# Moving blocks of conditioning work between the stages of a two-layer backbone kernel, with the conv's end started two jobs later, the gate row in another memory bank, and the output written in half as many stores

## The chip, the cores and the metric

The kernel runs on one core of a Trainium2 chip. The time is the device time of one execution in microseconds (us); lower is better. A core has five engines with a queue each: PE (TensorE, matrix products), DVE (VectorE), ACT (ScalarE), POOL (GpSimd) and SP (SyncE, which here only issues DMA transfers). An instruction waits at the head of its engine's queue until what it needs is there, and all behind it wait too.

## The reference

Two layers work on 256 latent tokens of width 2048, one sample. A conditioning vector c gives shift, scale and gate of each layer:

```
mod = silu(c) @ ada_w[layer] + ada_b[layer]          # 2048 -> 3 * 2048
shift, scale, gate = split(mod, 3)
h = rmsnorm(x, norm_g[layer]) * (1 + scale) + shift
# layer 0
k, v, q, za, glu, zb = split(h @ w_in)               # q, k: RMS norm and rotary
attn = attention of 8 query heads over latent and context keys
conv = silu(layernorm(depthwise_conv_31(a * sigmoid(b))))   # glu = a, b
x = x + gate * (concat(attn * silu(za), conv * silu(zb)) @ w_out0)
# layer 1
u, v, z = split(h @ w_in1);  x = x + gate * ((u * mix(layernorm(v)) * silu(z)) @ w_out1)
return rmsnorm(x, final_g)
```

All is fp32. The weights are far larger than the data of 256 tokens: 241 MB are read in one run.

## The kernel before, in words

**Jobs.** The work is a list of jobs (`plan`). A W job takes one piece of a weight matrix: 512 KB are loaded by SP into a buffer `raw`, ACT rounds it to `whi` (L389), DVE or, for the W jobs 30 to 133, POOL takes the rest `wlo = raw - whi` (L392), and PE multiplies both parts with both parts of the data, three products for each tile (`w_rows`, `w_cols`). In `w_cols` a job is twelve matmuls of 128x512. An adaLN vector of layer 0's shift and scale comes from PE (`araw`, L345).

**Conditioning blocks.** Gate 0 and all vectors of layer 1 are worked out on DVE instead: `adat_jobs` makes a job for each 512 KB block of the transposed `ada_w`; the block is loaded as `traw`, and two DVE instructions of 128x512 (L300) multiply it with the broadcast vector `cbp` (copied by L279 once for four blocks) and sum. There are 128 such blocks, hence 256 instructions of L300. The first 64 (`extra`: gate 0, then half of layer 1's shift and scale) run in layer 0, where two tables place them: `XTRA` says how many are woven into each of the five groups of stage one, `EX` how many into each of the seven segments after it. No matmul uses them at once; gate 0 is needed from the first output of `w_out0`.

**Loads.** `raw`, `araw` and `traw` share one ring of ten buffers. SP issues the loads in the jobs' order, twelve jobs ahead, each as soon as the buffer it is to fill has been released: a block that DVE has not yet worked on holds its buffer, and the loads behind it in SP's queue wait.

**Layer 0.** Stage one makes h in five groups of row blocks and multiplies at once (`glu_part`; L727 is the last step of the GLU half on DVE). Then come q, za (gate of the attention), z1 (gate of the conv, `z_part(1)`), `o0a` (the output projection over the attention's half, 16 jobs) and `o0b` (over the conv's half, 16 jobs). Attention steps and conv taps are side work: after each W job `drain` emits some of them, at a rate set by `PACE` for the conv. The conv's 31 taps for each of 8 channel blocks run on DVE (L664, L666) and accumulate in the one PSUM bank of tag "v"; ACT copies a finished pair out (L669).

**The conv's end** (`urgent`, appended by the hook `conv_tail`): `conv_mean` (matmuls `cmean`), `conv_centre` (`csum_p` on PE, L681 on DVE, squares on ACT), `conv_var` (`cvar`), `conv_root`, `conv_spread` (`csum_b`), and four `conv_fin` (L704, L707, L708, L483 and L484, which write `mBh` and `mBl`, the data of `o0b`). `crit["conv"]` is the last of these; `crit["crit"]` is the last early step of making a group's h (L512), or in layer 1 of its first half (L995). An instruction inside `after(key)` is placed behind that one on its engine. PE's order from q on is the order of the code (`inorder`).

**Gate row and outputs.** `gate_row` lays the gate out along the free axis: four times four matmuls into a bank `row_p` (L916) and an ACT copy (L918). `out_part` multiplies a finished accumulator by it (L930) and adds it to x (L931), both on DVE; the accumulators are three banks "a" and one "s". After `o0b` layer 1 begins with transposes `x1T` (L979). At the end `final` scales each 128-row chunk and stores it.

Of the kernel before, what the change touches and what calls it, by code (L numbers as in the profile page):

```python
# [13 lines left out]
AF = mybir.ActivationFunctionType  # L14
# [3 lines left out]
D = 2048  # L18
# [15 lines left out]
    SMALL[_n] = (_off, _w)  # L34
    _off += _w
SMALL_W = _off
BANKS = {"acc": "a", "S": "s", "conv": "v", "ada0": "v", "ada1": "s", "cbp": "c", "cvar": "v", "cfin": "v", "accx": "s", "row_p": "v"}
BUFS = {"a": 3, "s": 1, "v": 1, "m": 2, "c": 1}
ZG = ()
S0 = 3  # L40
# [20 lines left out]
SA = 4  # L61
P0 = 30
P1 = 134
PACE = 1.4
PACEA = 1.25
GROUPS = ((0, 2), (2, 2), (4, 4), (8, 4), (12, 4))
G = len(GROUPS)
# [1 line left out]
KVL = 0  # L69
BG = (1,)  # L70
G1 = 0
EX = (4, 4, 8, 8, 7, 9, 12)
XTRA = (0, 0, 4, 8, 0)
TSET = ((0, 4096), (0, 5120), (1, 0), (1, 2048), (1, 1024), (1, 3072), (1, 4096), (1, 5120))


# [9 lines left out]
def backbone_kernel(  # L86
# [24 lines left out]
    nc = tc.nc  # L111
# [128 lines left out]
    crit = {}  # L240

    def after(key):
        return tc.issue_after(crit[key]) if key in crit else nullcontext()

    pe = {"on": False}
# [35 lines left out]
    def adat_jobs(l, c0):  # L281

        js = []
        n = TSET.index((l, c0))
        res = tmp.tile([128, 8, 4], F32, tag="adat", name="adat", bufs=2)
        order = range(4) if n // 2 % 2 == 0 else range(3, -1, -1)
        for u, q in enumerate(order):
            for t in range(4):
                jb = Job()
                jb.kind = "A"  # L290

                def load(jb=jb, t=t, q=q):
                    jb.raw = ring.tile([128, 2, 512], F32, tag="raw", name="traw", bufs=RW)
                    ld(jb.raw, adat_d[n, q, t].rearrange("p (a b) -> p a b", a=2))

                def mm(jb=jb, t=t, q=q, u=u):
                    cb_part(q)
                    with after("crit" if "crit" in crit and l == 1 and c0 % D else "conv"):
                        for k in range(2):
                            nc.vector.scalar_tensor_tensor(  # L300
                                out=jb.raw[:, k, :], in0=jb.raw[:, k, :], scalar=1.0, in1=cbq["t"], op0=ALU.mult,
                                op1=ALU.mult, accum_out=res[:, 2 * t + k, q : q + 1])
                    if t == 3 and u == 3:
                        kind, k0 = c0 // D, (c0 % D) // 128
                        dst = modv[l][:, kind, k0 : k0 + 8]
                        nc.vector.tensor_reduce(out=dst, in_=res, axis=AX.X, op=ALU.add)
                        nc.vector.tensor_tensor(out=dst, in0=dst, in1=sm("ada_b", l * 48 + c0 // 128, 8), op=ALU.add)
                        if kind == 1:
                            nc.vector.scalar_tensor_tensor(out=dst, in0=dst, scalar=1.0,
                                                           in1=sm("norm_g", l * NKB + k0, 8), op0=ALU.add, op1=ALU.mult)  # L310
                        if kind == 0 and l == 1:
                            nc.vector.tensor_scalar(out=modn[:, k0 : k0 + 8], in0=dst, scalar1=-1.0, scalar2=None, op0=ALU.mult)
                jb.load, jb.split, jb.mm = load, lambda: None, mm
                js.append(jb)
        return js
# [144 lines left out]
    def hook(fn):  # L460
        jb = Job()
        jb.kind = "H"
        jb.load = jb.split = lambda: None
        jb.mm = fn
        return jb
# [58 lines left out]
    st = {}  # L524
# [396 lines left out]
    def gate_row(l):  # L921
        st["gate", l] = row_bcast(modv[l][:, 2], f"gate{l}")
# [169 lines left out]
    def final(i, r):  # L1092

        x, g = xt[i], st["fg"]

        def store(a, b):
            nc.sync.dma_start(out_d[i * 128 : (i + 1) * 128, a:b], x[:, a:b])
        nc.vector.scalar_tensor_tensor(out=x[:, 1536:], in0=x[:, 1536:], scalar=r, in1=g[:, 1536:], op0=ALU.mult, op1=ALU.mult)
        store(1536, 2048)
        for a in (0, 512):  # L1100
            nc.scalar.activation(x[:, a : a + 512], x[:, a : a + 512], AF.Copy, scale=r)
            store(a, a + 512)
        nc.vector.tensor_scalar(out=x[:, 1024:1536], in0=x[:, 1024:1536], scalar1=r, scalar2=None, op0=ALU.mult)
        store(1024, 1536)


    def need(key):
        jb = hook(lambda: drain(key))
        jb.key = key
        return jb  # L1110
# [12 lines left out]
    ada1 = adat_pair(1, 0, D)  # L1123
    extra = gate0 + ada1 if ORD == 0 else (ada1 + gate0 if ORD == 1 else weave(gate0, ada1))
    for g in range(G):
        body = glu_part(g)
        if g == 0:
            early = body[:NF]
        if g == KVL:
            body = [hook(load_ctx)] + body + [hook(statsc)]  # L1130
# [5 lines left out]
        if g == RT:  # L1136
            body = [hook(rope_tables)] + body
# [9 lines left out]
    o0b = out_part(w_out0, 0, hm, range(8, 16), True)  # L1147
    kv = [[hook(lambda: side["attn"].extend(attn_steps()))], [hook(lambda: st.__setitem__("q", True))]]
    za, (qa, qb) = z_part(0), q_part()
    segs = [body, [hook(load_xt), hook(lambda: pe.__setitem__("on", True))] + qa + za[:2] + kv[0] + za[2:4] + qb + [hook(lambda: st.__setitem__("rest", 4))], za[4:8] + kv[1] + za[8:] + [za_ready], z_part(1), [hook(lambda: gate_row(0)), need("attn")] + o0a[:4] + [conv_tail] + o0a[4:9], o0a[9:], [need("conv")] + o0b]  # L1150
    for seg, n in zip(segs, EX):
        plan += weave(seg, extra[:n])
        extra = extra[n:]
# [141 lines left out]
```

## Time and profile before

| what | value |
|---|---|
| three runs | 896.63, 890.85, 892.58 us, median 892.58 |
| the profiled execution | 891.98 us; its span, first to last instruction, 890.1 us |
| mean granted TensorE clock | 0.991 |
| busy share of the span | PE 95%, DVE 73%, ACT 51%, POOL 29% |
| stage one, to the last L727 | 0 to 214.6 us |
| q, za, z1 with attention and conv taps | 214.6 to 390.3 us |
| o0a, with the last taps and the conv's end | 390.3 to 446.2 us |
| o0b | 446.2 to 498.5 us |
| layer 1 | 500 to 880.7 us |
| end: last outputs and stores | 880.7 to 890.1 us |

The views of the profile used below are the page (busy time of each engine; groups of instructions with idle time and what released them; the chain of work that ended last), windows (busy time of each engine, the granted PE clock as a share of full speed, and the DMA engines' busy share in a stretch of time), waits (what an engine's instructions waited for), and timeline (single instructions; several equal ones in a row are joined, "x4"; a bracket gives the idle time before the instruction and what ended it). A busy PE is not PE at its peak, since its matmuls overlap: here the distance from start to start counts, 0.227 us for one of 128x512.

### The profile page before, as it was taken

The page shows a single profiled execution, that of the slowest core. Times are in us where ns is not written, and L with a number is a line of the kernel's source. Part 1 is how long each engine was busy: PE and PEld are TensorE (multiplying, and loading weights), DVE is VectorE, ACT ScalarE, POOL GpSimd, SP SyncE. Part 2 cuts the span into 40 slices and gives each one's busy share as a digit, 9 for nine tenths or more (in the row PEclk, how much of TensorE's full clock was granted, in tenths as well). Part 3 has the DMA queues.
Part 4 walks back from the last instruction along what each step waited for, and adds up shares of the span by engine and source line. Part 5 has one row for each costly group of instructions (what it writes and reads, how often), then busy time and mean ns, then how long its engine had stood idle before and what let it go on. Part 6 is the DMA issues. An engine that isn't in the chain of part 4 may idle for free.

```text
span 890.1 us, 14938 instructions
## 1 busy us (share of the span) xinstructions
PE 842.8 (95%) x5576; PEld 718.7 (81%) x5576; DVE 650.8 (73%) x1404; ACT 458.1 (51%) x689; POOL 256.6 (29%) x125
## 2 busy tenths in 40 slices
PE   5999999899989999998989899999999999899995
PEld 3787999899968989996868578878888888788884
DVE  2364783878788888884587599888999976555553
ACT  4643332555668777444635545456464444354452
POOL 0000013679864744785659520000000000000000
PEclk9999999999999999999999999999999999999998
DMA  9998998995765654585479689998987976665502
GB/s 350 405 396 311 393 364 330 410 369 194 243 245 177 214 184 165 190 305 168 166 275 409 262 306 409 404 349 323 306 304 272 353 259 213 235 216 177 197 25 95
DMA packets 67573, 244.10 MB, mean 274 GB/s; under 512 B 7582, under 2 KB 7848, under 8 KB 66348
## 3 DMA queue, kind: packets, MB, share of 16 engines
q1 hardware_dynamic: 67500, 243.14, 74.6%
q8 instruction: 44, 0.72, 0.3%
q14 instruction: 29, 0.24, 0.1%
HBM read 241.02 MB, written 2.10 MB: 273 GB/s over the span
## 4 chain that ended last, share of the span: by engine, by line
PE 58%; DVE 19%; DMA 13%; issue 4%; ACT 3%; POOL 2%; ACTq 0%; DVEq 0%; POOLq 0%; SPq 0%
PE acc L250 43%; DMA traw<-adat 8%; DVE traw L300 7%; PE accx L250 7%; DVE wlo L392 5%; PE ada L345 3%; POOL wlo L392 2%; DMA araw<-ada 2%; DVE conv L666 2%; DMA raw<-w_out 1%; PE O L250 1%; DMA raw<-w_uz 1%; ACT whi L389 1%; PE row_p L916 1%; PE x1T L979 1%
## 5 line engine op out<-in xcount | busy, mean ns | idle before, releaser
L389 ACT ACTIVATE whi<-raw 128x1024 fp32r<-128x1024 f32 (+1 forms) x256 | 263.3, 1032 | 251.1 <-PE acc L250 95.1
L392 POOL TENSOR_TENSOR wlo<-raw,whi 128x1024 fp32r<-128x1024 f32 x104 | 249.2, 2414 | 259.7 <-ACT whi L389 251.3
L392 DVE TENSOR_TENSOR wlo<-raw,whi 128x1024 fp32r<-128x1024 f32 (+1 forms) x152 | 176.7, 1168 | 81.9 <-ACT whi L389 81.4
L250 PE MATMUL acc<-h,whi 128*128 128x256 f32 x1024 | 190.8, 287 | 3.6 <-ACT whi L389 2.0
L300 DVE SCALAR_TENSOR_TENSOR traw<-traw,cbp 128x512 f32<-128x512 f32 x256 | 164.4, 685 | 37.7 <-DMA traw<-adat 36.6
L250 PEld LDWEIGHTS acc<-h,whi 128*128 128x128 f32 x1024 | 159.6, 192 | 8.5 <-ACT whi L389 2.8
L250 PE MATMUL acc<-h,wlo 128*128 128x256 f32 x512 | 144.6, 283 | 1.9 <-POOL wlo L392 1.9
L666 DVE SCALAR_TENSOR_TENSOR conv<-gaT,small,conv 128x241 f32<-128x241 f32 (+14 forms) x240 | 114.8, 478 | 5.4
L250 PE MATMUL acc<-wlo,h1h 128*128 128x512 f32 x288 | 114.7, 400 | 4.1 <-DVE wlo L392 3.9
L250 PE MATMUL acc<-whi,h1l 128*128 128x512 f32 x288 | 113.4, 396 | 0.4 <-DVE h1l L989 0.3
L250 PE MATMUL acc<-whi,h1h 128*128 128x512 f32 x288 | 108.3, 394 | 0.3 <-ACT whi L389 0.3
L250 PEld LDWEIGHTS acc<-h,wlo 128*128 128x128 f32 x512 | 98.0, 192 | 2.3 <-POOL wlo L392 2.3
L250 PE MATMUL acc<-whi,h 128*128 128x256 f32 (+1 forms) x256 | 68.0, 346 | 1.7 <-ACT z0T L641 1.7
L250 PEld LDWEIGHTS acc<-wlo,h1h 128*128 128x128 f32 x288 | 54.2, 188 | 17.0 <-DVE wlo L392 5.7
L250 PEld LDWEIGHTS acc<-whi,h1h 128*128 128x128 f32 x288 | 54.2, 188 | 12.8 <-ACT h1h L986 0.9
L250 PEld LDWEIGHTS acc<-whi,h1l 128*128 128x128 f32 x288 | 54.2, 189 | 12.4 <-DVE h1l L989 1.7
L250 PEld LDWEIGHTS acc<-whi,h 128*128 128x128 f32 x256 | 44.6, 190 | 8.6 <-ACT z0T L641 2.1
L250 PE MATMUL acc<-wlo,h 128*128 128x256 f32 (+1 forms) x128 | 43.3, 338 | 0.4 <-DVE wlo L392 0.4
L250 PE MATMUL accx<-whi,h1h 128*128 128x512 f32 x96 | 38.0, 396 | 0.0
L250 PE MATMUL accx<-wlo,h1h 128*128 128x512 f32 x96 | 38.0, 396 | 0.0
L250 PE MATMUL accx<-whi,h1l 128*128 128x512 f32 x96 | 37.9, 395 | 0.0
L250 PE MATMUL acc<-whi,m1h 128*128 128x512 f32 x96 | 37.6, 391 | 0.0
(257 smaller groups left out, 1284.5 us busy)
## 6 DMA issues: line engine op xcount, KB each, us to landing
traw<-adat SPq DMA_DIRECT2D x128, 512.0 KB, 5.6
raw<-w_out SPq DMA_DIRECT2D x64, 512.0 KB, 4.2
raw<-w_uz SPq DMA_DIRECT2D x64, 512.0 KB, 5.2
araw<-ada SPq DMA_DIRECT2D x56, 512.0 KB, 7.5
raw<-w_gate SPq DMA_DIRECT2D x56, 512.0 KB, 4.7
raw<-w_v SPq DMA_DIRECT2D x32, 512.0 KB, 6.7
raw<-w_q SPq DMA_DIRECT2D x16, 512.0 KB, 4.7
raw<-w_gate SPq DMA_DIRECT2D x16, 256.0 KB, 10.5
```

The lines of the kernel that those rows point to most:

```text
L250: i = op(*args, **kw)
L300: nc.vector.scalar_tensor_tensor(out=jb.raw[:, k, :], in0=jb.raw[:, k, :], scalar=1.0, in1=cbq["t"], op0=ALU.mult, op1=ALU.mult, accum_out ...
L345: nc.tensor.matmul(st8["p"][32 * g : 32 * g + 32, :w], ccol[:, kb, :], jb.raw[:, a, q * w : (q + 1) * w], start=kb < 4 // nq, stop=kb >= N ...
L389: nc.scalar.activation(hv, jb.raw, AF.Copy)
L392: eng.tensor_tensor(out=jb.lo.rearrange("p a b -> p (a b)"), in0=jb.raw, in1=hv.bitcast(F32), op=ALU.subtract)
L666: nc.vector.scalar_tensor_tensor(out=o, in0=y, scalar=w, in1=o, op0=ALU.mult, op1=ALU.add)
L916: nc.tensor.matmul(pb[:, b * 128 : (b + 1) * 128], vec[:, 4 * q + b : 4 * q + b + 1].broadcast_to([128, 128]), ident, start=True, stop=True)
L979: nc.tensor.matmul(p[:, k, c * 128 - c0 : c * 128 - c0 + 128], xt[c][:, (k0 + k) * 128 : (k0 + k + 1) * 128], st["diag", c], start=True, s ...
```

## The change

- `XTRA`: stage one gets 2 and 4 conditioning blocks in its third and fourth groups, where it had 4 and 8. The six blocks, and some of the later ones, are spread anew by `EX`: 3, 6, 9, 8, 8, 9, 15 blocks in the seven segments instead of 4, 4, 8, 8, 7, 9, 12.
- L298: a block's DVE work is placed behind `crit["crit"]` throughout. Before, most blocks were placed behind the conv's end once its last step had been emitted.
- `conv_tail` is appended after the sixth job of `o0a` instead of the fourth, and `PACE` is 2.2 instead of 1.4.
- `row_p` uses the tag "m" (two banks) instead of "v" (one, which the conv's taps hold).
- `final` scales the first 1024 columns in one ACT instruction instead of two, and stores a chunk in two transfers of 1024 columns instead of four of 512. The first of chunk 1 is issued on ACT's queue, the others on SP's.

```diff
--- before.py
+++ after.py
@@ -34,7 +34,7 @@
     SMALL[_n] = (_off, _w)
     _off += _w
 SMALL_W = _off
-BANKS = {"acc": "a", "S": "s", "conv": "v", "ada0": "v", "ada1": "s", "cbp": "c", "cvar": "v", "cfin": "v", "accx": "s", "row_p": "v"}
+BANKS = {"acc": "a", "S": "s", "conv": "v", "ada0": "v", "ada1": "s", "cbp": "c", "cvar": "v", "cfin": "v", "accx": "s", "row_p": "m"}
 BUFS = {"a": 3, "s": 1, "v": 1, "m": 2, "c": 1}
 ZG = ()
 S0 = 3
@@ -61,7 +61,7 @@
 SA = 4
 P0 = 30
 P1 = 134
-PACE = 1.4
+PACE = 2.2
 PACEA = 1.25
 GROUPS = ((0, 2), (2, 2), (4, 4), (8, 4), (12, 4))
 G = len(GROUPS)
@@ -69,8 +69,8 @@
 KVL = 0
 BG = (1,)
 G1 = 0
-EX = (4, 4, 8, 8, 7, 9, 12)
-XTRA = (0, 0, 4, 8, 0)
+EX = (3, 6, 9, 8, 8, 9, 15)
+XTRA = (0, 0, 2, 4, 0)
 TSET = ((0, 4096), (0, 5120), (1, 0), (1, 2048), (1, 1024), (1, 3072), (1, 4096), (1, 5120))
 
 
@@ -295,7 +295,7 @@
 
                 def mm(jb=jb, t=t, q=q, u=u):
                     cb_part(q)
-                    with after("crit" if "crit" in crit and l == 1 and c0 % D else "conv"):
+                    with after("crit"):
                         for k in range(2):
                             nc.vector.scalar_tensor_tensor(
                                 out=jb.raw[:, k, :], in0=jb.raw[:, k, :], scalar=1.0, in1=cbq["t"], op0=ALU.mult,
@@ -1093,15 +1093,13 @@
 
         x, g = xt[i], st["fg"]
 
-        def store(a, b):
-            nc.sync.dma_start(out_d[i * 128 : (i + 1) * 128, a:b], x[:, a:b])
+        def store(eng, a, b):
+            eng.dma_start(out_d[i * 128 : (i + 1) * 128, a:b], x[:, a:b])
         nc.vector.scalar_tensor_tensor(out=x[:, 1536:], in0=x[:, 1536:], scalar=r, in1=g[:, 1536:], op0=ALU.mult, op1=ALU.mult)
-        store(1536, 2048)
-        for a in (0, 512):
-            nc.scalar.activation(x[:, a : a + 512], x[:, a : a + 512], AF.Copy, scale=r)
-            store(a, a + 512)
         nc.vector.tensor_scalar(out=x[:, 1024:1536], in0=x[:, 1024:1536], scalar1=r, scalar2=None, op0=ALU.mult)
-        store(1024, 1536)
+        nc.scalar.activation(x[:, :1024], x[:, :1024], AF.Copy, scale=r)
+        store(nc.scalar if i else nc.sync, 0, 1024)
+        store(nc.sync, 1024, 2048)
 
 
     def need(key):
@@ -1147,7 +1145,7 @@
     o0b = out_part(w_out0, 0, hm, range(8, 16), True)
     kv = [[hook(lambda: side["attn"].extend(attn_steps()))], [hook(lambda: st.__setitem__("q", True))]]
     za, (qa, qb) = z_part(0), q_part()
-    segs = [body, [hook(load_xt), hook(lambda: pe.__setitem__("on", True))] + qa + za[:2] + kv[0] + za[2:4] + qb + [hook(lambda: st.__setitem__("rest", 4))], za[4:8] + kv[1] + za[8:] + [za_ready], z_part(1), [hook(lambda: gate_row(0)), need("attn")] + o0a[:4] + [conv_tail] + o0a[4:9], o0a[9:], [need("conv")] + o0b]
+    segs = [body, [hook(load_xt), hook(lambda: pe.__setitem__("on", True))] + qa + za[:2] + kv[0] + za[2:4] + qb + [hook(lambda: st.__setitem__("rest", 4))], za[4:8] + kv[1] + za[8:] + [za_ready], z_part(1), [hook(lambda: gate_row(0)), need("attn")] + o0a[:6] + [conv_tail] + o0a[6:9], o0a[9:], [need("conv")] + o0b]
     for seg, n in zip(segs, EX):
         plan += weave(seg, extra[:n])
         extra = extra[n:]
```

**DVE at the end of the conv.** L666 are the last taps, L681 subtracts the mean from the conv's result. Before:

```order
L666 SCALAR_TENSOR_TENSOR conv<-gaT,small,conv 128x245
L666 SCALAR_TENSOR_TENSOR conv<-gaT,small,conv 128x244
L666 SCALAR_TENSOR_TENSOR conv<-gaT,small,conv 128x243
L666 SCALAR_TENSOR_TENSOR conv<-gaT,small,conv 128x242
L666 SCALAR_TENSOR_TENSOR conv<-gaT,small,conv 128x241
L930 TENSOR_TENSOR acc<-acc,gate_4872 128x512 x2
L931 TENSOR_TENSOR xt_2861<-acc,xt_2861 128x512
L931 TENSOR_TENSOR xt_2863<-acc,xt_2863 128x512
L681 TENSOR_TENSOR gaT<-gaT,csum_p 128x512 x4
L930 TENSOR_TENSOR acc<-acc,gate_4872 128x512
L931 TENSOR_TENSOR xt_2861<-acc,xt_2861 128x512
L930 TENSOR_TENSOR accx<-accx,gate_4872 128x512
```

and with the change:

```order
L300 SCALAR_TENSOR_TENSOR traw,adat<-traw,cbp 128x512 x2
L666 SCALAR_TENSOR_TENSOR conv<-gaT,small,conv 128x243
L279 COPY cbp<-cb 128x512
L666 SCALAR_TENSOR_TENSOR conv<-gaT,small,conv 128x242
L300 SCALAR_TENSOR_TENSOR traw,adat<-traw,cbp 128x512 x2
L666 SCALAR_TENSOR_TENSOR conv<-gaT,small,conv 128x241
L300 SCALAR_TENSOR_TENSOR traw,adat<-traw,cbp 128x512 x2
L681 TENSOR_TENSOR gaT<-gaT,csum_p 128x512 x4
L300 SCALAR_TENSOR_TENSOR traw,adat<-traw,cbp 128x512 x2
L930 TENSOR_TENSOR acc<-acc,gate_4856 128x512
L300 SCALAR_TENSOR_TENSOR traw,adat<-traw,cbp 128x512 x2
L930 TENSOR_TENSOR accx<-accx,gate_4856 128x512
```

Blocks (L300, two instructions each) now stand between the last taps and around L681, where before there were none. Somewhat earlier, among the last ten taps, the first outputs of `o0a` (L930, L931) stand before the conv's end as well, where before they stood behind it:

```order
L300 SCALAR_TENSOR_TENSOR traw,adat<-traw,cbp 128x512 x2
L666 SCALAR_TENSOR_TENSOR conv<-gaT,small,conv 128x252
L300 SCALAR_TENSOR_TENSOR traw,adat<-traw,cbp 128x512 x2
L666 SCALAR_TENSOR_TENSOR conv<-gaT,small,conv 128x251
L930 TENSOR_TENSOR acc<-acc,gate_4856 128x512
L666 SCALAR_TENSOR_TENSOR conv<-gaT,small,conv 128x250
L930 TENSOR_TENSOR acc<-acc,gate_4856 128x512
L931 TENSOR_TENSOR xt_2841<-acc,xt_2841 128x512
L666 SCALAR_TENSOR_TENSOR conv<-gaT,small,conv 128x249
L931 TENSOR_TENSOR xt_2843<-acc,xt_2843 128x512
L300 SCALAR_TENSOR_TENSOR traw,adat<-traw,cbp 128x512 x2
```

From the last L727 to the last tap DVE has 76 instructions of L300, 214 taps, 4 copies L279 and two L930 and L931 each; before, 52, 212, 2 and none. Behind the last L861 (the last of the attention's products on DVE) the counts are 32 of L300 and 53 taps, and were 12 and 48.

**PE around the mean of the conv.** `cmean` sums the conv's result over channels; `mAh` and `mAl` are the attention's data, so these matmuls are jobs of `o0a`. Before:

```order
L250 MATMUL accx<-wlo,mAh 128x512
L250 MATMUL accx<-whi,mAl 128x512
L250 MATMUL cmean<-gaT,onesC 32x256 x8
L916 MATMUL row_p<-ident,modv_133 128x128 x4
L250 MATMUL acc<-whi,mAh 128x512
L250 MATMUL acc<-wlo,mAh 128x512
L250 MATMUL acc<-whi,mAl 128x512
```

and, two jobs later, still before the change:

```order
L250 MATMUL accx<-wlo,mAh 128x512
L916 MATMUL row_p<-ident,modv_133 128x128 x4
L250 MATMUL accx<-whi,mAl 128x512
L250 MATMUL accx<-whi,mAh 128x512
L250 MATMUL accx<-wlo,mAh 128x512
L250 MATMUL accx<-whi,mAl 128x512
L916 MATMUL row_p<-ident,modv_133 128x128 x8
L250 MATMUL cvar<-csq,onesC 32x256 x8
```

and with the change:

```order
L250 MATMUL accx<-whi,mAh 128x512
L250 MATMUL accx<-wlo,mAh 128x512
L250 MATMUL accx<-whi,mAl 128x512
L250 MATMUL cmean<-gaT,onesC 32x256 x8
L250 MATMUL csum_p<-csum,q_126 128x256
L250 MATMUL acc<-whi,mAh 128x512
L250 MATMUL acc<-wlo,mAh 128x512
```

Before, five jobs of `o0a` stood ahead of `cmean` and the gate row behind it in three places, the last one right ahead of `cvar`. Now seven jobs and the whole gate row stand ahead of `cmean`, `csum_p` follows it at once, and `cvar` comes one job later.

**DVE behind the conv's last step** (L484, which writes `mBl`). Before:

```order
L484 TENSOR_TENSOR mBl<-cfin,mBh 128x512
L300 SCALAR_TENSOR_TENSOR traw,adat<-traw,cbp 128x512 x4
L279 COPY cbp<-cb 128x512
L300 SCALAR_TENSOR_TENSOR traw,adat<-traw,cbp 128x512 x14
L930 TENSOR_TENSOR acc<-acc,gate_4872 128x512 x2
L300 SCALAR_TENSOR_TENSOR traw,adat<-traw,cbp 128x512 x2
L931 TENSOR_TENSOR xt_2861<-acc,xt_2861 128x512
L931 TENSOR_TENSOR xt_2863<-acc,xt_2863 128x512
L279 COPY cbp<-cb 128x512
L300 SCALAR_TENSOR_TENSOR traw,adat<-traw,cbp 128x512 x6
L930 TENSOR_TENSOR acc<-acc,gate_4872 128x512
```

and with the change:

```order
L708 TENSOR_TENSOR cfin<-cfin,z1T 128x512
L300 SCALAR_TENSOR_TENSOR traw,adat<-traw,cbp 128x512 x2
L931 TENSOR_TENSOR xt_2843<-accx,xt_2843 128x512
L484 TENSOR_TENSOR mBl<-cfin,mBh 128x512
L300 SCALAR_TENSOR_TENSOR traw,adat<-traw,cbp 128x512 x4
L306 TENSOR_REDUCE modv_134<-adat 128x8
L307 TENSOR_TENSOR modv_134<-modv_134,small 128x8
L312 TENSOR_SCALAR modn<-modv_134 128x8
L930 TENSOR_TENSOR acc<-acc,gate_4856 128x512
L931 TENSOR_TENSOR xt_2841<-acc,xt_2841 128x512
L300 SCALAR_TENSOR_TENSOR traw,adat<-traw,cbp 128x512 x2
```

Before, 36 instructions of L300 stood between the last L484 and the first `x1T` of layer 1, now 12.

## The prediction

> **What bounds the kernel now.** I read the page first: which engine is busy, and which chain ended last.
>
> ```profile
> PE 842.8 (95%) x5576; PEld 718.7 (81%) x5576; DVE 650.8 (73%) x1404; ACT 458.1 (51%) x689; POOL 256.6 (29%) x125
> PE 58%; DVE 19%; DMA 13%; issue 4%; ACT 3%; POOL 2%; ACTq 0%; DVEq 0%; POOLq 0%; SPq 0%
> L300 DVE SCALAR_TENSOR_TENSOR traw<-traw,cbp 128x512 f32<-128x512 f32 x256 | 164.4, 685 | 37.7 <-DMA traw<-adat 36.6
> L666 DVE SCALAR_TENSOR_TENSOR conv<-gaT,small,conv 128x241 f32<-128x241 f32 (+14 forms) x240 | 114.8, 478 | 5.4
> ```
>
> PE is busy 95% of the span, so what the change can win is what PE idles, stage by stage. The blocks' DVE work (L300) waits 36.6 us for its loads, which matters only where DVE is late. Next the stretches that the change touches: the end of stage one, q to z1, the last taps, the rest of o0a, and o0b.
>
> ```profile
> core 0: us, PE busy (x) PEld busy (x) DVE busy (x) ACT busy (x) POOL busy (x), PEclk, DMA share, GB/s
> 100.00:158.00 58.00, 58.00 (x758) 54.99 (x758) 36.75 (x75) 16.55 (x24) 10.50 (x5) 1.00 0.94 355
> 158.00:187.00 29.00, 26.09 (x211) 25.28 (x210) 21.89 (x59) 16.84 (x24) 21.96 (x10) 1.00 1.02 410
> 214.60:365.20 150.60, 146.56 (x923) 127.16 (x922) 129.03 (x329) 104.80 (x188) 94.74 (x40) 1.00 0.60 206
> 365.20:406.20 41.00, 39.88 (x284) 36.58 (x282) 33.67 (x76) 17.90 (x20) 34.45 (x14) 1.00 0.75 263
> 406.20:446.20 40.00, 37.47 (x194) 30.38 (x195) 19.71 (x37) 23.09 (x34) 22.26 (x10) 1.00 0.45 147
> 446.20:498.50 52.30, 46.73 (x193) 36.73 (x191) 38.09 (x104) 25.13 (x37) 38.70 (x17) 0.97 0.91 358
> ```
>
> PE has no gap from 100 to 158, and 2.9 us of gaps (29.00 - 26.09) from 158 to 187, with the DMA engines full (1.02). The largest loss is in o0b: its 192 matmuls at 0.227 us from start to start need 43.6 us, and it took 52.3, so 8.7 are lost. The waits of PE, for 158 to 187, for 400 to 446 and for 446 to 500, say on what:
>
> ```profile
> PE acc L250 <- POOL wlo L392: 1.9, 2, 1.3
> PE acc L250 <- ACT whi L389: 1.0, 2, 0.8
> ...
> PE row_p L916 <- ACT gate L918: 1.9, 2, 1.2
> PE cmean L250 <- ACT gaT L669: 1.1, 1, 1.1
> PE cvar L250 <- ACT gate L918: 0.7, 1, 0.7
> ...
> PE acc L250 <- POOL wlo L392: 5.5, 4, 1.9
> ```
>
> And the chain of waits from 440 on shows why POOL is late in o0b:
>
> ```profile
> 445.09 1.30 DVE traw L300 x4
> 446.41 4.21 DMA raw<-w_out
> ...
> 460.50 4.34 DVE traw L300 x15
> ...
> 469.09 2.33 DVE traw L300 x7
> 471.42 8.50 DMA raw<-w_out
> ...
> 480.61 1.92 POOL wlo L392
> ```
>
> Blocks that stand behind the conv's end hold buffers of the ring; when DVE gets to them the loads of w_out start, too late for POOL's split.
>
> **The change part by part.** The sum is made against the profiled execution's 891.98 us: a span of 890.1 and 1.9 around it. The median shown is 892.58, 0.6 more. A measurement of this kernel can tell about 1% (8.9 us) from no change.
>
> *Prices.* The timeline gives the steps:
>
> ```profile
> 452.91 0.68 DVE L300 SCALAR_TENSOR_TENSOR traw<-traw,cbp 128x512 f32<-128x512 f32 x1
> ...
> 453.51 0.68 DVE L300 SCALAR_TENSOR_TENSOR traw<-traw,cbp 128x512 f32<-128x512 f32 x1
> ...
> 395.73 9.80 DVE L666 SCALAR_TENSOR_TENSOR conv<-gaT,small,conv 128x252 f32<-128x252 f32 x19
> 405.56 0.58 ACT L669 COPY gaT<-conv 128x512 f32<-128x512 f32 x1 [3.04 <-DVE conv L666]
> 406.20 0.63 PE L250 MATMUL cmean<-gaT,onesC 128*32 128x256 f32 x4 [1.12 <-ACT gaT L669]
> ...
> 412.77 1.05 PE L916 MATMUL row_p<-ident,modv 128*128 128x128 f32 x8
> 413.58 0.48 PE L250 MATMUL accx<-whi,mAl 128*128 128x512 f32 x1
> ```
>
> An L300 follows the other by 0.61 us, so a block takes DVE 1.2; a tap 0.51 (9.80 / 19); L279, L930 and L931 0.69 each (the group of o0b has 0.688, 0.696 and 0.683). The conv's taps end at 405.53, ACT copies, PE goes on at 406.20, 0.67 later; its wait of 1.12 means that it was ready at 405.08. A quarter of the gate row takes PE 0.81 (412.77 to 413.58).
>
> *(a) End of stage one.* Six blocks, so 3 MB of loads and 7.3 us of DVE work, leave groups three and four. Only the 2.9 us of PE's gaps, 1.9 of them on POOL and 1.0 on ACT, can go; from 100 to 158 PE hides everything. But the last vectors' jobs of the groups stand later in PE's order now, with less work between them and the h that needs them, and L300 behind `crit` moves too. Bounds -3.2 (all gaps and a little of the next stretch) and +1.5 (half the gain lost to a new gap of the size of the longest, 1.3). I take half the gaps: **-1.5**.
>
> *(b) Conv end and cmean.* By the order, DVE has 24 more L300 (14.6 us), 2 more taps (1.0), 2 more L279 (1.4) and 4 more L930 and L931 (2.8) before the last tap: 19.8 us. Of these 0.9 lie ahead of the last attention product, where DVE idled 21.6 us in 150.6 and waited among the rest for loads; that hides them. The other 18.9 fall where DVE has 7.3 us idle (41.00 - 33.67), of it 5.2 in waits for loads (of DVE, 214.6 to 365.2, then 365.2 to 406.2):
>
> ```profile
> DVE traw L300 <- DMA traw<-adat: 11.9, 14, 2.6
> ...
> DVE traw L300 <- DMA traw<-adat: 5.2, 4, 1.8
> ```
>
> A DVE that is later than the loads doesn't wait for them: where blocks stood close together, in o0b, 37 L300 waited 1.7 us in one wait. I take 0.9 + 5.2 = 6.1 as hidden; the bounds are 8.2 (all idle time) and -8.7 (each of the ten added blocks waits as the six did there, 5.2 / 6 = 0.87, and nothing is hidden). Taps end at 405.53 - 1.5 + 19.8 - 6.1 = 417.7 and PE goes on at 418.4, 12.2 later. Ahead of `cmean` PE now does two more jobs (2 x 12 x 0.227 = 5.4) and the gate row (4 x 0.81 = 3.2), 8.6 that it no longer does behind. So (a) and (b) together are 12.2 - 8.6 = **+3.6**. PE is ready at 405.08 - 1.5 + 8.6 = 412.2, so it stands 6.2 us at `cmean`. Behind it in PE's queue are the rest of o0a and o0b; ACT and POOL fill their four split buffers meanwhile.
>
> *(c) Gate row and the conv's end.* The waits of `row_p` and `cvar` for the one bank, 1.9 + 0.7 = 2.6, go: the gate row runs at o0a's start from two other banks. New: `csum_p` stands right behind `cmean` and needs ACT's copy first, 0.8 (a 0.58 copy and hand-overs); `cvar` has one job (2.7) ahead, while L681 four times (2.8) and ACT's last square (0.6) take 3.7 with hand-overs, so 1.0; `csum_b` has one job ahead again and its reciprocal stands on DVE behind six L300 and four L930 and L931 (6.4 us), so 2.5. Sum 4.3 - 2.6 = **+1.7**, bounds -2.6 and +4.3.
>
> *(d) PE's clock.* After a gap in o0b the granted clock fell:
>
> ```profile
> 454.29 0.80 PE L250 MATMUL acc<-wlo,mBh 128*128 128x512 f32 x1 [1.94 <-POOL wlo L392]
> ...
> 454.00:458.00 4.00, 3.71 (x9) 2.98 (x10) 3.88 (x12) 0.00 (x0) 2.57 (x2) 0.57 0.63 224
> ```
>
> 0.57 for 4 us is 1.7 us lost; a stand of 6.2 us should bring it once: **+1.7**, bounds 0 and 3.4 (twice). [...]
>
> *(e) o0b.* Only 12 L300 instead of 36 stand between the conv's last step and layer 1, and blocks before it are released as they come. If w_out's loads are in time, the gaps (6.7) and the fall of the clock (1.7) go, of 8.7 in all. POOL limits the gain: 38.70 us busy must fit into 43.6. I leave 1.0: **-7.7**, bounds -8.7 and 0.
>
> *(f) The stores.* The end before:
>
> ```profile
> 881.48 4.92 SPq L1097 DMA_DIRECT2D out_dram<-xt  x8
> 883.85 1.33 ACT L1101 ACTIVATE xt<-xt,ss 128x512 f32<-128x512 f32 x2 [0.23 <-DVE ss L235]
> ```
>
> Eight issues take SP 4.92 us, 0.6 each; now three and one run side by side. But the first half goes out only after the whole ACT step, 0.6 later than its first half did, and 2 MB must still move: **+0.2**, bounds -0.6 and +0.8. [...]
>
> *Sum:* +3.6 + 1.7 + 1.7 - 7.7 + 0.2 = -0.5, so **891.5 us**.
>
> **The rivals.**
>
> *R1, slower: loads pace the conv.* Each added block waits for its load like those from 365 on, and DVE hides none of its lateness: (b) rises by 6.1 + 8.7 = 14.8, to **906.3**. For it: L300 waited in 18 places up to 406, and a late DVE keeps ring buffers, which delays the next loads. Against: the DMA engines have room there (0.60 and 0.75). It decides from 10.0 us above the forecast's conv end, 427.7: then the kernel is over 1% slower.
>
> *R2, faster: DVE catches up.* All of DVE's idle time takes up the new work, and stage one's gaps vanish: taps end at 405.53 - 3.2 + 18.9 - 7.3 = 413.9, PE goes on at 414.6, so (a) and (b) are 8.4 - 8.6 = -0.2; with (c) and (d) as above, (e) -8.7 and (f) -0.3 the sum is -5.8, **886.2**; without the new waits of (c) it would be 881.9. For it: DVE's 21.6 us idle before 365. Against: the added work stands behind them.
>
> *R3, the change doesn't do what it says in o0b.* DVE is late at the conv's end itself, so blocks still hold the ring there, and POOL, at 2.4 us for a split of 2.7, never catches up: (e) is 0 and the time **899.2**. For it: 8 L300 now stand between L681 and L704, and 9 blocks in the o0a segment. Against: DVE's 19.71 of 40.00 after 406 leaves room.
>
> **How the numbers follow.** Forecast 0.46, with its own range 885 to 899; R2 0.28, R1 0.16, R3 0.10. The range to hold 8 in 10 takes most of R2 and the lower half of R1: 882 to 906. Bounds of 1% around 892.58 are 883.7 and 901.5. Faster: two fifths of R2 (its case without new waits, 0.11) and a little of the forecast, 0.19. Slower: nearly all of R1 (0.14), a third of R3 and a little of the forecast, 0.19. Within: 0.62.
>
> **What would show it.** Right: the last tap near 418 and a wait of `cmean` for L669 of 5 to 9 us; no wait of `row_p`; waits at `cvar` and `csum_b`; a stretch of granted clock near 0.57 behind `cmean`; o0b in 44 to 46 us without `wlo` waits; stores ending as far behind the last matmul as before, 9.4 us. Wrong: `cmean` without a wait of PE (R2), many waits of L300 between the taps (R1), `wlo` waits in o0b as before (R3), or a change of more than 3 us outside 158 to 500, which no step here has.

## The result, and the profile after

The changed kernel takes 901.61 us (median of five, 899.59 to 903.07), the kernel before 892.58 (890.85 to 896.73): the ratio is 1.0095, 95% interval 1.0067 to 1.0123. It is slower by about 1%, where 891.5 was forecast with an upper end of the range at 906. The profiled execution took 903.07, the highest of its five, with a span of 901.3 against 890.1. So the stages below add up to 11.2 us, while the medians differ by 9.0.

The page of the changed kernel, its first lines and the group of the blocks:

```profile
span 901.3 us, 14918 instructions
PE 846.2 (94%) x5576; PEld 722.0 (80%) x5576; DVE 659.3 (73%) x1404; ACT 457.4 (51%) x686; POOL 256.2 (28%) x125
L300 DVE SCALAR_TENSOR_TENSOR traw<-traw,cbp 128x512 f32<-128x512 f32 x256 | 164.4, 681 | 56.9 <-DMA traw<-adat 56.4
```

The blocks' own work is unchanged (164.4 us); their waits for loads went from 36.6 to 56.4. Windows of the changed kernel, cut at its own landmarks (last L727, last L861, last tap, o0b):

```profile
core 0: us, PE busy (x) PEld busy (x) DVE busy (x) ACT busy (x) POOL busy (x), PEclk, DMA share, GB/s
158.00:187.00 29.00, 28.57 (x268) 27.50 (x267) 22.47 (x53) 16.25 (x25) 21.36 (x10) 1.00 0.92 359
212.98:369.42 156.44, 149.31 (x923) 130.02 (x922) 134.75 (x335) 105.17 (x187) 94.20 (x40) 0.98 0.61 209
369.42:428.85 59.43, 49.29 (x342) 45.01 (x340) 49.15 (x125) 24.05 (x27) 41.49 (x17) 0.94 0.80 280
429.50:433.50 4.00, 3.51 (x10) 2.17 (x11) 1.97 (x6) 0.84 (x2) 0.00 (x0) 0.50 0.91 329
433.50:437.50 4.00, 4.00 (x27) 2.54 (x26) 4.00 (x11) 2.92 (x5) 0.00 (x0) 0.78 0.24 62
...
463.00:510.10 47.10, 44.83 (x194) 35.80 (x192) 28.27 (x60) 23.44 (x36) 37.27 (x17) 1.00 0.76 273
```

PE's gaps at the end of stage one are nearly gone (29.00 - 28.57 = 0.4 us, before 2.9), and o0b takes 46.9 us instead of 52.3 (the last row above begins with the last matmul of o0a). But the conv's last tap comes at 428.85 instead of 405.53, and PE stands idle for it. PE's waits, from 214 to 365, from 400 to 446 and from 446 on:

```profile
PE ktp L250 <- ACT kT L802: 3.2, 1, 3.2
PE acc L250 <- DVE qr L767: 2.8, 1, 2.8
...
PE cmean L250 <- ACT gaT L669: 10.8, 1, 10.8
PE csum_b L250 <- DVE rs L235: 2.8, 1, 2.8
PE csum_p L250 <- ACT csum L198: 0.5, 1, 0.5
...
PE acc L250 <- POOL wlo L392: 2.3, 3, 1.3
```

The place on the timelines of DVE, ACT and PE, with the last tap, its copy, and the matmul that waited:

```profile
428.38 0.47 DVE L666 SCALAR_TENSOR_TENSOR conv<-gaT,small,conv 128x241 f32<-128x241 f32 x1
...
428.88 0.59 ACT L669 COPY gaT<-conv 128x512 f32<-128x512 f32 x1 [8.49 <-DVE conv L666]
...
429.52 1.07 PE L250 MATMUL cmean<-gaT,onesC 128*32 128x256 f32 x4 [10.80 <-ACT gaT L669]
```

From the landmarks of the two profiled executions, times in us:

| landmark | before | after | later by |
|---|---|---|---|
| last L727 (end of stage one) | 214.57 | 212.98 | -1.6 |
| last L861 (end of the attention's products) | 365.22 | 369.42 | +4.2 |
| last tap | 405.53 | 428.84 | +23.3 |
| first matmul of o0b | 446.21 | 463.24 | +17.0 |
| last matmul of o0b | 498.53 | 510.11 | +11.6 |
| last matmul of all | 880.71 | 892.03 | +11.3 |
| end of the span | 890.12 | 901.28 | +11.2 |

The loss is made between the last L727 and the first matmul of o0b; o0b returns 5.4 of it; layer 1 and the stores change by 0.3 and 0.15.

### The profile page after: what moved, and what is told of

Same layout as the page of the kernel before. It is cut to its first block, busy times and chain, and to the rows that moved or that the text cites. A ratio compares the mean times of both kernels' runs of the same rounds, so it can differ in the third digit from the quotient of the medians.

```text
span 901.3 us, 14918 instructions
## 1 busy us (share of the span) xinstructions
PE 846.2 (94%) x5576; PEld 722.0 (80%) x5576; DVE 659.3 (73%) x1404; ACT 457.4 (51%) x686; POOL 256.2 (28%) x125
## 4 chain that ended last, share of the span: by engine, by line
PE 51%; DVE 17%; DMA 11%; issue 10%; POOL 9%; ACT 1%; DVEq 0%; POOLq 0%; SPq 0%; ACTq 0%
PE acc L250 37%; POOL wlo L392 9%; DMA traw<-adat 8%; PE accx L250 6%; DVE traw L300 6%; DVE wlo L392 4%; PE ada L345 3%; DMA araw<-ada 1%; PE O L250 1%; PE x1T L979 1%; DVE ht L502 1%; DVE conv L666 1%; DMA cin<-ccol 1%; DVE v L1034 1%; PE ptp L250 0%
## 5 line engine op out<-in xcount | busy, mean ns | idle before, releaser
L300 DVE SCALAR_TENSOR_TENSOR traw<-traw,cbp 128x512 f32<-128x512 f32 x256 | 164.4, 681 | 56.9 <-DMA traw<-adat 56.4
L250 PE MATMUL acc<-h,whi 128*128 128x256 f32 x1024 | 193.3, 289 | 5.5 <-DVE qr L767 2.8
L250 PEld LDWEIGHTS acc<-h,whi 128*128 128x128 f32 x1024 | 161.0, 193 | 11.4 <-issue 3.4
L666 DVE SCALAR_TENSOR_TENSOR conv<-gaT,small,conv 128x241 f32<-128x241 f32 (+14 forms) x240 | 114.5, 477 | 4.9
## 6 DMA issues: line engine op xcount, KB each, us to landing
raw<-w_gate SPq DMA_DIRECT2D x16, 256.0 KB, 10.8
```

The lines of the kernel that those rows point to most:

```text
L250: i = op(*args, **kw)
L300: nc.vector.scalar_tensor_tensor(out=jb.raw[:, k, :], in0=jb.raw[:, k, :], scalar=1.0, in1=cbq["t"], op0=ALU.mult, op1=ALU.mult, accum_out ...
L666: nc.vector.scalar_tensor_tensor(out=o, in0=y, scalar=w, in1=o, op0=ALU.mult, op1=ALU.add)
```

## The experiments

**Theory 1**, after the result: the conv's end is set by DVE's own work in the order behind the last L861; the blocks put there delay it one for one, and PE stands at `cmean`. **Theory 2**: loads pace DVE; blocks wait for 512 KB that come late through the ring, and the work itself matters little.

### e1: blocks held behind the conv's end again

```diff
-                    with after("crit"):
+                    with after("crit" if "crit" in crit and l == 1 and c0 % D else "conv"):
```

> The changed kernel with one thing undone: blocks are again placed behind the conv's end once its last step has been emitted. By the order, 14 L300 and 56 taps then stand between the last L861 and the last tap, instead of 32 and 53, so 18 x 0.61 - 3 x 0.51 = 9.5 us less DVE work there, and 44 L300 behind the conv's last step instead of 12. Theory 1 (DVE's own work behind the last L861 sets the conv's end, one for one): last tap at about 419.3 instead of 428.8, PE's wait at cmean down from 10.8 to about 1, o0b loses again some 5 us of what it won; 895 to 899 us. Theory 2 (loads that come late through the ring of ten buffers pace DVE): the last tap comes only 2 to 4 us earlier and o0b is worse; 902 to 906 us.

Measured: 904.44 us, ratio 1.0103 (1.0052 to 1.0154). The last tap came 47.7 us behind the last L861 instead of 59.4, so 11.7 less, near the 9.5 of theory 1, and PE had no wait at `cmean`. The time, though, lies in theory 2's range and 5 us above theory 1's. What was forecast too small is the price of the hold: o0b took 61.5 us.

```profile
PE acc L250 <- POOL wlo L392: 6.5, 4, 1.9
PE acc L250 <- ACT whi L389: 3.4, 3, 1.9
```

These are PE's waits in o0b: both halves of the split are late, and the granted clock was 0.89 in the windows of o0b. That the held blocks keep the ring is read from the chain of e6 below. The wait at `cmean` and the hold's cost in o0b lose about as much: the ratio is 1.0103 here and 1.0095 in the changed kernel.

### e2: the old tables

```diff
-EX = (3, 6, 9, 8, 8, 9, 15)
-XTRA = (0, 0, 2, 4, 0)
+EX = (4, 4, 8, 8, 7, 9, 12)
+XTRA = (0, 0, 4, 8, 0)
```

> The changed kernel with the old tables of blocks (12 blocks in stage one, 4, 4, 8, 8, 7, 9, 12 behind it). By the order, 25 L300 and 48 taps stand between the last L861 and the last tap instead of 32 and 53: 6.8 us less DVE work; stage one gets back 1.6 us. Theory 1: last tap about 7 us earlier against the last L861 and PE's waits for rope and attention (3.2 and 2.8 us) back to before's; 890 to 895 us. Theory 2: as many blocks wait for loads in layer 0, so the waits of L300 stay near 28 us from 214 to the last tap; 898 to 902 us.

Measured: 896.82 us, ratio 1.0037 (1.0005 to 1.0068). The last tap came 52.65 us behind the last L861, 6.8 less than in the changed kernel, as theory 1 had it. That it fits to the tenth is luck: DVE was busy 5.2 us less, and the rest is shorter waits. Theory 2 had the waits of L300 from 214 to the last tap stay near 28 us; they are 25.4 in the changed kernel and 20.2 here. The time is 2 us above theory 1's range and below theory 2's: 4.5 us of the wait at `cmean` are left.

### e3: the blocks of o0a moved into o0b

```diff
-EX = (3, 6, 9, 8, 8, 9, 15)
+EX = (3, 6, 9, 8, 0, 8, 24)
```

> The changed kernel with the eight blocks of o0a's first segment and one of the second moved to o0b (0, 8, 24 blocks in the last three segments). By the order, 6 L300 and 51 taps between the last L861 and the last tap instead of 32 and 53, so 16.9 us less DVE work there; 20 L300 instead of 8 between the last tap and L704, 18 behind the conv's last step instead of 12. Theory 1: last tap near 412, no wait of PE at cmean, but longer waits at csum_b (5 to 8 us); 889 to 895 us. Theory 2: the loads of blocks fall together in o0b, splits wait there again and o0b loses 5 us or more; 897 to 902 us.

Measured: 891.81 us, ratio 0.9986 (0.9953 to 1.0019): the whole loss is gone. The last tap came at 401.3, and `cmean` did not wait. The waits of L300 were 34.2 us from 214 to 512, nearly as many as in the changed kernel (38.3), so their total does not set the time; between the last L861 and the last tap they fell from 9.0 to 4.3. The waits at `csum_p`, `csum_b` and for `mBh` were 2.0, 2.8 and 2.7 us.

### e4: half of the blocks' multiplication left out

```diff
-                                out=jb.raw[:, k, :], in0=jb.raw[:, k, :], scalar=1.0, in1=cbq["t"], op0=ALU.mult,
+                                out=jb.raw[:, k, :w], in0=jb.raw[:, k, :w], scalar=1.0, in1=cbq["t"][:, :w], op0=ALU.mult,
```

with w = 256 for the blocks of layer 0 and 512 for the others.

> The changed kernel, whose blocks of layer 0 multiply only the first 256 of 512 columns (half of the product is left out); loads and order as in the changed kernel. An L300 of layer 0 then takes about 0.3 us less. Theory 1: DVE has 32 x 0.3 = 9.6 us less behind the last L861 and as much ahead; last tap near 417, PE's wait at cmean 0 to 2 us, waits for rope gone; 886 to 892 us. Theory 2: DVE waits for the loads instead; the waits of L300 grow by most of the time saved and the gain is under 4 us; 897 to 901 us.

Measured: 892.19 us, ratio 0.9982 (0.9960 to 1.0004). One condition of the expectation was false: the program's order of instructions depends on how long the instructions are taken to be, and with shorter ones 33 taps and 12 L300 stood behind the last L861 instead of 53 and 32. The last tap came at 391.3, far earlier than 417. The waits for blocks from 214 to 512 rose to 53.1 us, as theory 2 had it, and the time fell by 9.4 us, as theory 1 had it. Since the order changed too, this run does not tell DVE's work from the loads.

### e5, e6, e7: the edits alone on the kernel before

e5 takes only the hold away, e6 has only the new tables (the diffs of e1 and e2, turned round, on the kernel before). e7 has all the rest:

```diff
-"row_p": "v"}
+"row_p": "m"}
-PACE = 1.4
+PACE = 2.2
-o0a[:4] + [conv_tail] + o0a[4:9]
+o0a[:6] + [conv_tail] + o0a[6:9]
```

and the stores of the changed kernel.

> The kernel before with one edit: no block is held behind the conv's end (L298). By the order, 24 L300 and 48 taps stand between the last L861 and the last tap, where the kernel before has 12 and 48, and 8 instead of 36 behind the conv's last step. Theory 1 (DVE's work behind the last L861 sets the conv's end, one for one): last tap 7.3 us later against the last L861, 47 to 51 us behind it instead of 40.3, PE's wait at cmean 8 to 11 us instead of 1.1, o0b about 5 us shorter; 894 to 898 us. Rival, theory 3 (taking the hold away costs nothing, and the loss comes from the tables of blocks): no longer wait at cmean, o0b shorter; 886 to 890 us.

> The kernel before with the new tables of blocks alone (six blocks fewer in stage one). By the order, 14 L300 and 56 taps between the last L861 and the last tap, before 12 and 48; 42 L300 instead of 36 behind the conv's last step, held there. Theory 1: 5.3 us more DVE work behind the last L861, last tap 45 to 48 us behind it, PE's wait at cmean 5 to 8 us; o0b longer by 3 to 9 us, since more held blocks keep buffers of the ring; stage one at most 1.6 us shorter; 899 to 906 us. Rival: the six blocks taken from stage one win more there than they cost, 886 to 891 us.

> The kernel before with all edits but the tables and the hold: the gate row in two banks, PACE 2.2, the conv's end two jobs later, two stores a chunk. By the order, DVE has the same 12 L300 and 48 taps behind the last L861, and PE two jobs and the gate row more ahead of cmean. Theory 1: no wait at cmean, none of the gate row; small new waits at csum_p and csum_b; o0b as before (52 us); the stores worth 0.1 us; 889 to 893 us. Rival: the later start of the conv's end makes mBl late and o0b waits for it; 895 to 899 us.

Measured: e5 900.6 us, ratio 1.0074 (1.0039 to 1.0108); e6 905.62, 1.0137 (1.0104 to 1.0170); e7 893.46, 0.9989 (0.9964 to 1.0013). In e5 PE waited 8.7 us at `cmean` and o0b took 48.0 us instead of 52.3, both about as theory 1 had them; the median is 2.6 us above its range. Theory 3 falls. In e6 the time is in theory 1's range; PE waited 4.9 us at `cmean`, and o0b took 61.0 us with the same waits as in e1:

```profile
PE acc L250 <- POOL wlo L392: 6.5, 4, 1.9
PE acc L250 <- ACT whi L389: 3.4, 3, 1.9
```

The chain of e6 shows loads of w_out that start when DVE has worked on held blocks, and the splits that follow them:

```profile
450.81 1.31 DVE traw L300 x4
452.13 4.53 DMA raw<-w_out
456.77 1.06 ACT whi L389
...
466.49 1.92 DVE traw L300 x7
468.43 6.40 DMA raw<-w_out
474.93 1.07 ACT whi L389
```

So the new tables are bad with the hold (o0b) and bad without it (the conv). The rest by itself changes nothing that can be measured; e7 is 0.5 us above its range. It may help once the hold is gone: PE waited 4.5 us at `cmean` in e2, which has it, and 8.7 in e5, which has not, but the intervals of the two ratios overlap.

### e8: e3 with the conv's end started after the fourth job of o0a

```diff
-EX = (3, 6, 9, 8, 8, 9, 15)
+EX = (3, 6, 9, 8, 0, 8, 24)
-o0a[:6] + [conv_tail] + o0a[6:9]
+o0a[:4] + [conv_tail] + o0a[4:9]
```

> The changed kernel with the blocks of o0a moved to o0b (0, 8, 24 in the last three segments) and the conv's end started after the fourth job of o0a again. By the order, 6 L300 and 51 taps between the last L861 and the last tap, 14 L300 instead of 20 from there to L704. Theory 1: last tap near 401, so cmean waits little after five jobs; against the run with the sixth job (891.8, last PE instruction at 880.9 us) the waits for mBh (2.7 us) go and csum_p's stay: 886 to 891 us. Theory 2: the blocks' loads fall together in o0b, where splits wait 3 us or more; 892 to 896 us.

Measured: 889.44 us, ratio 0.9947 (0.9917 to 0.9977): faster than both kernels, than the one before by half a per cent. Against e3 (0.9953 to 1.0019) the intervals overlap, so the earlier start of the conv's end is not shown to win. Its stretch from the last L861 to the last tap:

```profile
core 0: us, PE busy (x) PEld busy (x) DVE busy (x) ACT busy (x) POOL busy (x), PEclk, DMA share, GB/s
367.86:402.93 35.07, 35.07 (x273) 33.99 (x272) 29.55 (x66) 16.22 (x19) 26.58 (x11) 1.00 0.56 193
```

PE has no gap here, where the changed kernel's row above has 10.1 us (59.43 - 49.29), and the whole conv's end up to o0b has one wait of 2.0 us left, at `csum_p`. In o0b PE waits 1.7 and 1.3 us for `mBl` and `mBh`, and no longer for splits.

### e9 to e12: the rate of the taps, and the size of the ring

Theory P: taps put in faster delay the attention. e9 is the changed kernel, e12 is e8, with this edit:

```diff
-PACE = 2.2
+PACE = 1.4
```

Theory R: the size of the ring sets the waits of L300. e10 and e11 are the changed kernel with another number of buffers; e11 has one buffer of the tag t2 fewer to make room:

```diff
-RW = 10
+RW = 9     (e10)
+RW = 11    (e11)
-TB = 9
+TB = 8     (e11)
```

> The changed kernel with PACE 1.4 again instead of 2.2 (the rate at which conv taps are put behind each W job). Over the runs so far the stretch from the last L727 to the last L861 took 150.7 to 151.0 us in three runs with 1.4 and 150.9 to 156.4 in six with 2.2. Theory P (taps put in faster stand ahead of rope and softmax on DVE and delay the attention): that stretch goes from 156.4 to about 151, the waits for rope and kT (3.2 and 2.8 us) shrink, 896 to 899 us. Rival (only scatter between executions): the stretch may come out anywhere between, the time stays at 900 to 903 us. By the order the stretch behind the last L861 is as in the changed kernel (32 L300, 53 taps), so the last tap comes 57 to 60 us behind it in both.

> The changed kernel with nine buffers instead of ten in the ring of loads. By the order, 30 L300 and 52 taps between the last L861 and the last tap (32 and 53 in the changed kernel). Theory R (a block that DVE has not worked on keeps its buffer, so DVE's lateness comes back as late loads): L300 waits there longer, 12 to 16 us instead of 9.0, and the last tap comes no earlier; 904 to 910 us. Rival (the waits are the DMA engines' own pace, 0.80 busy there): waits 8 to 10 us, 899 to 902 us.

> The changed kernel with eleven buffers in the ring of loads (and eight instead of nine buffers of the tag t2, which makes the room). By the order, 34 L300 and 56 taps between the last L861 and the last tap, so 2.7 us more DVE work there. Theory R: L300 waits there 4 to 7 us instead of 9.0, and less ahead of it, so the last tap comes no later in spite of the added work; 897 to 901 us. Rival (DMA's own pace): waits 8 to 10 us, last tap 2 to 3 us later, 902 to 905 us.

> The fastest kernel so far (no blocks in o0a's first segment, the conv's end after the fourth job) with PACE 1.4. By the order, 6 L300 and 51 taps behind the last L861 as there, 18 L300 instead of 14 from the last tap to L704. Theory P: the attention ends 2 us earlier, o0a with it, 886 to 889 us. Rival (scatter): 888 to 892 us, against 889.4 for that kernel.

Measured: e9 904.67 us, ratio 1.0121 (1.0085 to 1.0157); e10 902.71, 1.0111 (1.0068 to 1.0155); e11 902.91, 1.0100 (1.0061 to 1.0140); e12 889.64, 0.9968 (0.9940 to 0.9996). Theory P falls: the stretch from the last L727 to the last L861 took 151.7 us in e9, as P had it, but 158.4 in e12, the longest of all and with the same PACE, and the time of e9 did not fall: it is above both ranges (its o0b took 56.2 us, with waits of 7.8 for `mBh`). The size of the ring does little behind the last L861: L300 waited 10.7 us there with nine buffers, 9.0 with ten, 8.8 with eleven, though for 15, 16 and 17 blocks. Theory R had 12 to 16 and 4 to 7; the rival had 8 to 10, which fits eleven and misses nine by 0.7. The time of e10 lies between the two ranges, that of e11 in the rival's. Elsewhere the ring did matter: with nine buffers stage one ended at 220.2 us, where nine other runs with these tables ended it at 214.1 on average, and later stretches made up for most of it.

### What the runs show together

The stretch from the last L861 to the last tap, from the order (L300 and taps) and each run's windows and waits, in us:

| run | L300 | taps | length | DVE busy | L300 waits | PE's wait at cmean |
|---|---|---|---|---|---|---|
| e4 (L300 halved) | 12 | 33 | 29.3 | 21.2 | 7.2 | 0 |
| e8 | 6 | 51 | 35.1 | 29.6 | 3.9 | 0 |
| e12 | 6 | 51 | 35.3 | 29.5 | 4.2 | 0 |
| e3 | 6 | 51 | 35.4 | 29.5 | 4.3 | 0 |
| e7 | 12 | 48 | 37.8 | 33.3 | 3.2 | 0 |
| before | 12 | 48 | 40.3 | 33.7 | 5.2 | 1.1 |
| e6 | 14 | 56 | 44.5 | 37.3 | 5.5 | 4.9 |
| e1 | 14 | 56 | 47.7 | 39.4 | 6.8 | 0 |
| e5 | 24 | 48 | 47.8 | 40.8 | 5.7 | 8.7 |
| e2 | 25 | 48 | 52.6 | 43.9 | 7.6 | 4.5 |
| e10 | 30 | 52 | 58.7 | 46.8 | 10.7 | 11.8 |
| after | 32 | 53 | 59.4 | 49.2 | 9.0 | 10.8 |
| e9 | 32 | 53 | 60.0 | 49.2 | 9.6 | 11.4 |
| e11 | 34 | 56 | 62.1 | 51.8 | 8.8 | 13.4 |

From e8 to the changed kernel DVE's busy time grows by 19.6 us and the stretch by 24.3: 1.24 us for each us of work. The added blocks cost their own time, DVE's idle time grows with them from 5.5 to 10.3 us, and nothing is absorbed. So work is four fifths of the growth and waiting one fifth: theory 1 holds in the main, but not one for one. A block that is moved takes its load along, so this division is read from the traces; no run changed the one without the other.

## Why the prediction was wrong, point by point

**(a), the end of stage one, was right**: -1.6 measured, -1.5 forecast. Nine profiled executions with the new tables (ten buffers or eleven) end it at 214.1 on average, four with the old ones at 215.8. They scatter by 2.8 us among the nine and 2.1 among the four, so the agreement of the one pair to 0.1 is luck.

**But it was given back at once**, and this is the first step that failed: the prediction carries the -1.5 on to the last tap ("Taps end at 405.53 - 1.5 + 19.8 - 6.1"), leaves 0.9 us of added work to DVE's idle time before the last L861, and has no term for waits of PE there. The transposes of the keys (`ktp`) wait for ACT's `kT`, and ahead of it ACT's queue stood 2.7 us for DVE's L777, part of the rope work. A shorter stage one does not bring this forward: the first `kT` was copied at 247.29 here, and at 247.07 in e3, where stage one ended 2.1 us later. PE waited 3.2 us there, 0.6 in the kernel before. At 298.31 PE waited 2.8 us for the rope of q (L767, 0.6 before). Behind both stands the granted clock fell, where the kernel before has 1.00 in the same windows:

```profile
246.00:250.00 4.00, 2.29 (x7) 1.77 (x8) 3.93 (x11) 3.95 (x8) 2.53 (x2) 0.69 0.46 163
250.00:254.00 4.00, 4.00 (x20) 3.08 (x19) 3.81 (x11) 2.74 (x6) 2.22 (x2) 0.89 0.74 269
...
298.00:302.00 4.00, 3.69 (x19) 3.72 (x20) 3.81 (x12) 3.52 (x5) 4.00 (x3) 0.59 0.61 193
```

That is 4 x (0.31 + 0.11 + 0.41) = 3.3 us of clock. The chain to the second stand leads back to a block:

```profile
281.04 6.68 DMA traw<-adat
...
287.82 1.30 DVE traw L300 x4
...
297.84 0.34 DVE qr L767
298.18 0.14 issue
298.31 1.74 PE acc L250 x8
```

A block in front of the rope on DVE waited for its load. This alone does not explain the stand, since in the kernel before the chain passes through a block's load at the same place (5.13 us from 290.93). The last L861 is 4.2 us later, where the prediction had it 1.5 earlier. How much of these 5.7 us belongs to the change is not settled: with the same order of PE and nearly the same of DVE up to there, e3 and e8 took 150.9 and 153.1 us from the last L727 to the last L861, the changed kernel 156.4. Of all fourteen profiled executions three had a clock below 1.00 in this stretch, the changed kernel (0.98), e11 (0.99) and e12 (0.96), and they are the three longest, 156.4 to 158.4 us against 149.1 to 153.8. So a good part of the 5.7 may be this one execution's clock.

**(b) is the step that failed most clearly**: "I take 0.9 + 5.2 = 6.1 as hidden". From the last L861 to the last tap DVE was to be busy 33.65 + 18.9 = 52.6 us, with 6.7 - 5.2 = 1.5 idle. It was busy 49.2 and idle 10.3. So the idle time was 8.8 too small in the forecast and the work 3.4 too large, and the sum was off by 5.4 only because the two errors have opposite signs. (One L279 was added, not two, and the one L484 in the stretch took 1.2 us instead of 2.6.) The waits for loads did not go, they grew from 5.2 to 9.0 us:

```profile
DVE traw L300 <- DMA traw<-adat: 9.0, 9, 3.1
```

The reason given, that a late DVE finds its loads there, holds only for the later part. Three of the nine waits, 6.3 us in all, end by 396, before most of the added blocks:

```profile
374.48 0.69 DVE L300 SCALAR_TENSOR_TENSOR traw<-traw,cbp 128x512 f32<-128x512 f32 x1 [0.51 <-DMA traw<-adat]
...
381.45 0.69 DVE L300 SCALAR_TENSOR_TENSOR traw<-traw,cbp 128x512 f32<-128x512 f32 x1 [2.66 <-DMA traw<-adat]
...
395.82 0.69 DVE L300 SCALAR_TENSOR_TENSOR traw<-traw,cbp 128x512 f32<-128x512 f32 x1 [3.08 <-DMA traw<-adat]
```

Behind them ten more blocks wait six times, 0.2 to 0.9 us each and 2.7 in all. The chain of the early part shows how blocks wait for each other:

```profile
369.81 1.22 DVE traw L300 x4
371.04 3.42 DMA traw<-adat
374.48 1.30 DVE traw L300 x4
375.78 0.03 DVE conv L666
375.81 5.62 DMA traw<-adat
381.45 1.32 DVE traw L300 x4
382.78 3.52 DMA traw<-adat
```

In this chain a load is issued when a block has been worked on and left its buffer, and a later block waits for that load, so a DVE that comes late makes loads late. SP's waits for L300 from the last L861 to the last tap went from 8.0 to 21.5 us:

```profile
SPq L122 <- DVE traw L300: 21.5, 15, 2.6
```

Only the chain argues for this loop; no run shows it, and that a buffer more or less leaves the waits nearly the same (e10, e11) stays unexplained. The prediction took its reason from o0b, where 37 L300 waited 1.7 us in one wait; those blocks were held there until the conv's end, so their loads may have landed long before; no run here settles this.

The last tap came at 428.84, forecast 417.7; 5.7 of the 11.1 come from the attention, 5.4 from this step. It lies 1.1 beyond R1's point of decision (427.7), and the kernel is slower by about 1%. The rival R1, with a chance of 0.16, was right that DVE hides nothing; but the waits grew by 3.8 us where it priced 8.7, and without the attention's 5.7, which R1 did not have, the last tap would have come at 423.1. That its point was passed is in part luck.

**PE's stand at `cmean`** was 10.8 us, forecast 6.2: the last tap came 11.1 us late, and PE itself was ready 6.5 late, at 418.7 instead of 412.2, most of it from the attention. The later PE shortens the stand but not the time, which the last tap sets.

**(c) and (d) were right in sum.** From the matmul that waited at `cmean` to o0b lay 33.7 us, forecast 34.8. The waits of the gate row are gone, `csum_b` waits 2.8 (2.5 forecast), `csum_p` 0.5 (0.8), `cvar` not at all (1.0). Behind the stand the clock was at 0.50 for 4 us and at 0.78 for the next 4, which is 2.9 us by the windows where 1.7 was forecast. So the sum was better than its terms.

**(e) was right in kind, too large in size**: -5.4 instead of -7.7. `wlo` waits of 2.3 us remain of 5.5, where 1.0 was left for all. That the hold was the cause is shown by e5, 48.0 us without it, and by e1 and e6, where more held blocks make o0b 61 us long.

**(f)**: the end behind the last matmul went from 9.41 to 9.25 us, forecast +0.2. One pair of executions does not tell this from no change.

## What to carry to other kernels

Before the change DVE and PE came to the conv's end within half a us of each other (405.53 and 405.08): where two engines meet like that, work put on the later one's path cost its full time here and somewhat more (1.24 us for each us, from e8 to the changed kernel), and idle time on that path was not room, since it consisted mostly of waits for loads (5.2 of 6.7 us before, 9.0 of 10.3 after) that the added work did not shorten. In this kernel work that nothing needs soon belongs behind the meeting point, neither ahead of it (e5) nor held until the conv's last step (e6): moving the blocks behind it turned +0.95% into -0.14% (e3), level with the kernel before, and with an earlier start of the conv's end into -0.53% (e8). What stage one won, 1.6 us, was lost behind it: the next chain did not start earlier with it (the first `kT` at 247.29, and at 247.07 in e3, where stage one ended 2.1 us later).

## What had not been expected of the hardware

Two waits of equal length at the same matmul left the clock in different states. In the changed kernel PE waited 2.8 us for L767 until 298.31, and the clock fell; in e8 it waited 2.8 us for L767 too, until 297.79 (300 less the 2.21 us that PE is busy from 296 to 300), and the clock did not fall. The same window behind the two is 0.59 in the changed kernel (its row stands above) and 1.00 in e8:

```profile
298.00:302.00 4.00, 4.00 (x28) 3.49 (x28) 3.82 (x13) 3.93 (x6) 4.00 (x2) 1.00 0.56 184
```

In the kernel before, the clock fell after a shorter wait, of 1.94 us until 454.29: it was 0.57 from 454 to 458. So in these three executions the length of the wait alone does not tell whether the clock falls, and no run shows what else decides it. The mean granted clock goes along with the scatter between executions of the same program: of the eleven of e12 the slowest, 900.71 us, had the lowest, 0.975, and one of 888.38 had 0.991. Which is cause and which effect these two numbers do not show.
